# GpSimd without arithmetic in the expert blocks of a two-block transformer

## Chip, core and metric

The kernel runs on one core of one Trainium2 chip. The metric is the device time of one execution in microseconds (us). Engines are named as in the profile: PE (TensorE, matrix products), DVE (VectorE), ACT (ScalarE), POOL (GpSimd) and SP (SyncE, which only issues transfers). PEclk is the granted clock of PE as a share of full speed.

## What is computed

A first block (two layers of three token mixers and a feed-forward of width 2816, on 256 tokens of width 1024) is followed by a second block of two layers. Each of these holds an attention of the 256 latent tokens, together with 256 context tokens, and an expert layer with 16384 experts. Everything is in float32.

```
first_block, per layer:  x += concat(rwkv7(h), dilated(h), mla(h)) @ w_out
                         x += (silu(h @ w_gate) * (h @ w_up)) @ w_down        # h = rms_norm(x)
second_block, per layer: x += g1 * attention(...) @ w_o
                         x += g2 * peer_ffn(h2)                               # latents
  layer 0 only:          xc += cg2 * peer_ffn(h2c)                            # context

def peer_block(hb, w_q, sub_keys, u_tab, v_tab):
    q1, q2 = halves of (hb @ w_q) per head                    # 8 heads
    v1, i1 = top_k(q1 @ sub_keys[0].T, 16); v2, i2 = top_k(q2 @ sub_keys[1].T, 16)
    top_s, pos = top_k(v1[:, None] + v2[None, :], 16)         # 16 of 256 pairs
    expert = (i1 * 128 + i2)[pos];  g = softmax(top_s)
    u = u_tab[expert]                                         # 128 rows per token
    w = g * gelu(einsum('nhkd,nd->nhk', u, hb))
    return einsum('nhk,nhkd->nd', w, v_tab[expert])
```

## The kernel before

**Products.** A float32 product is made of three PE products of parts: a tensor is split into `hi` (ACT, L177) and `lo = src - hi` (L181), and `mm3` (L184 to L191) adds hi*hi, hi*lo and lo*hi. `split` puts the subtraction on VectorE or, with `eng2="g"`, on GpSimd.

**Feed-forward (`ffn`, L509).** For each of 22 tiles of the width, gate and up products, then the activation (`ffact`, L526). A second loop over the 22 tiles splits the activation (`ffak`, hi on ACT and lo on GpSimd, L540) and half of the tiles of `w_down` on VectorE and GpSimd in turn (L538), and accumulates into four banks of PSUM.

**Experts of the context tokens (`peer_gather`, L1394), layer 0.** For each of two blocks of 128 tokens there are 128 gathers of u rows (`ug`, L1425; each brings 128 rows of 4 KB), each followed by a dot product with `hm`: on GpSimd and ACT (L1415 and L1416) or as one operation on VectorE (L1418). `dot` chooses: in block 0 the first 60 and every third after the 118th go to GpSimd, in block 1 every third. Then 128 gathers of v rows (`vg`, L1449) feed small products `pv` (L1454). This work runs beside the second feed-forward, attention 0 and the layer 0 experts of the latents. The u rows pass through four buffers, from the 174th on through two.

**Experts of the latents (`Dense`, L1500).** All 16384 experts are computed for all 256 tokens, in parts (four of 32 tiles in layer 0, two of 64 in layer 1), and weighted by a mostly empty matrix. `u_part`: a tile `u_raw` is loaded, split (hi on ACT L1564, lo by columns on GpSimd and VectorE L1567: 256 of 1024 columns on GpSimd in the first two parts of layer 0, 512 in the others), multiplied (`aT`, L1580 to L1582), and passed through gelu to `d_A`. `w_part`: one-hot matrices `o` (L1621, L1623) and `og` (L1626) on VectorE, a product `gps` on PE (L1630), and the result multiplied into `d_A` (L1632). `v_part`: a tile `v_raw` is loaded and split (hi on ACT L1649, lo half on GpSimd L1650 and half on VectorE L1651), a row of `d_A` is split (`w_hi`, `w_lo`, L177 and L181), and PE accumulates `acc` (L1664). `mesh` interleaves the loops. In layer 0 the order is u0 with the routing, u1 beside w0, v0 beside w1, u2, v1 beside w2, u3, v2 beside w3, v3. In layer 1 it is u0 with the routing, u1 beside w0, v0 beside w1, v1.

**Order.** A scheduler places the instructions of each engine by priorities (`n.rank`, `issue_after`) and its own model of time. Every engine runs its list in order: an instruction that waits holds all behind it on its engine. Gathers stand in POOL's list, loads of tiles in SP's.

Names that the prediction uses: `qn` (L1171) is a normalised query of attention 0, `h2xv` (L1097) belongs to the norm that ends attention 0, `d_gT` (L1603) is the end of the routing.

Of the kernel before, what the change touches and what calls it, by code (L numbers as in the profile page):

```python
# [10 lines left out]
F32 = mybir.dt.float32  # L11
F32R = mybir.dt.float32r
# [4 lines left out]
AF = mybir.ActivationFunctionType  # L17
ALU = mybir.AluOpType
# [3 lines left out]
P = 128  # L22
D = 1024
S = 256
KD = D // P
L = 2
DFF = 2816
KF = DFF // P
# [216 lines left out]
def part(pair, *idx):  # L245
    return tuple(t[(slice(None),) + idx] for t in pair)
# [51 lines left out]
class First:  # L298
# [207 lines left out]
                xs = x[:, b, hf * 512 : (hf + 1) * 512]  # L506
                nc.vector.tensor_tensor(xs, pss[hf][b], xs, op=ALU.add)

    def ffn(self, l, x, after=None, more=None):  # L509

        nc, n, a = self.nc, self.n, self.a
        hT, _ = self.norm_T(x, self.vcol("ffn_norm_g", l, 8), "hT2")
        if after:
            after()
        act = self.zones["x"].tile([P, KF, S], F32, name="ffact")
        for c in range(KF):
            ps = self.psum("pgu")
            for i, name in enumerate(("ffn_w_gate", "ffn_w_up")):
                w = self.w.load(a[name][l, c], KD, P, "wgu")
                for k in range(KD):  # L520
                    n.mm3(ps[:, i * S : (i + 1) * S], part(w, k), part(hT, k), k == 0, k == KD - 1)
            th = self.t([P, S], "ffth")
            nc.scalar.activation(th, ps[:, :S], AF.Tanh, scale=0.5)
            nc.vector.tensor_scalar(th, th, 0.5, 0.5, op0=ALU.mult, op1=ALU.add)
            nc.vector.tensor_tensor(th, ps[:, :S], th, op=ALU.mult)
            nc.vector.tensor_tensor(act[:, c], ps[:, S:], th, op=ALU.mult)  # L526
        wd = a["ffn_w_down"][l].rearrange("(k p) c -> p k c", p=P)
        pss = [self.psum(f"pd{i}") for i in range(4)]
        for k in range(KF):
            ws = self.w if more is None or k % 2 else more  # L530
            if k % 4 < 2:
                w = part(ws.load(wd[:, k : k + 1], 1, D, "wd"), 0)
            else:
                if k % 2 == 0:
                    two = self.zones["x"].pair([P, 2, D], "wd2")
                w = part(two, k % 2)
                raw = ws.plain(wd[:, k : k + 1], 1, D, "wd")
                n.split(raw[:, 0], *w, eng2="gv"[k % 2])  # L538
            ak = self.z.pair([P, S], "ffak")
            n.split(act[:, k], *ak, eng2="g")  # L540
            for b in range(2):
                for hf in range(2):
                    n.mm3(pss[2 * b + hf], part(ak, slice(b * P, (b + 1) * P)), part(w, slice(hf * 512, (hf + 1) * 512)), k == 0, k == KF - 1)
        for b in range(2):
            for hf in range(2):
                xs = x[:, b, hf * 512 : (hf + 1) * 512]
                nc.vector.tensor_tensor(xs, pss[2 * b + hf], xs, op=ALU.add)
# [438 lines left out]
class Second:  # L986
# [408 lines left out]
    def peer_gather(self, slots, rows, out, gp, vp, act0, hm0):  # L1395
# [3 lines left out]
        n, nc = self.n, self.nc  # L1399
# [7 lines left out]
        def u_rows(b):  # L1407
            hm = self.t([P, D], "hm") if b else hm0
            nc.gpsimd.dma_start(hm, rows[b])
            act = self.t([P, P], "act") if b else act0  # L1410

            def dot(j, u):
                o = act[:, j : j + 1]
                if j < EARLY if b == 0 and j < EARLY + GATHERS else j % POOL_DOTS == 0:
                    nc.gpsimd.tensor_tensor(u, u, hm, op=ALU.mult)  # L1415
                    nc.scalar.activation(u, u, AF.Copy, accum_out=o)  # L1416
                else:
                    nc.vector.tensor_tensor_reduce(out=u, in0=u, in1=hm, scale=1.0, scalar=0.0, op0=ALU.mult, op1=ALU.add, accum_out=o)  # L1418

            for j in range(P):  # L1420
                if b == 0 and j == SOON:
                    hm = self.t([P, D], "hm")
                    nc.gpsimd.dma_start(hm, rows[b])
                u = row(j, "ug")
                nc.gpsimd.indirect_dma_start(out=u, out_offset=None, in_=ut, in_offset=bass.IndirectOffsetOnAxis(ap=slots[b][0][:, j : j + 1], axis=0))  # L1425
                dot(j, u)
                yield
            gl = self.gelu(act, [P, P], "ga")
            w = self.t([P, P], "gw_")
            nc.vector.scalar_tensor_tensor(w, gl, 0.5, slots[b][2][:, b], op0=ALU.mult, op1=ALU.mult)  # L1430
            ps = self.psumt()
            nc.tensor.transpose(ps[:, 0:P], w, n.ident)
            wTs[b] = self.t([P, P], "wT")
            nc.scalar.activation(wTs[b], ps[:, 0:P], AF.Copy)
# [68 lines left out]
class Dense:  # L1503
# [9 lines left out]
    def __init__(self, net, ctx, x, h, l, col, parts, banks, raw):  # L1513
        tc = net.tc
        self.n, self.nc, self.a = net, net.nc, net.a
        self.x, self.l, self.col = x, l, col
        self.hh, self.hl = h
        self.pw, self.pr = None, raw
        self.parts = parts
        self.low = ((2, 2, 4, 4), (4, 4))[l]  # L1520
        self.first = [sum(parts[:i]) for i in range(len(parts))]
        self.pa = ctx.enter_context(tc.tile_pool(name=f"d_a{l}", bufs=1, reuse_waits="tile"))
        self.i = 0
        self.pr2 = None if l else ctx.enter_context(tc.tile_pool(name=f"d_s{l}", bufs=RAWS, reuse_waits="tile"))
        self.pu = ctx.enter_context(tc.tile_pool(name=f"d_u{l}", bufs=2 if l else SPLITS, reuse_waits="tile"))
        self.po = ctx.enter_context(tc.tile_pool(name=f"d_o{l}", bufs=2, reuse_waits="tile"))
        self.pp = ctx.enter_context(tc.tile_pool(name=f"d_p{l}", bufs=banks, space=PSUM, reuse_waits="tile"))
# [26 lines left out]
    def u_part(self, f, A):  # L1554
        nc, n, H = self.nc, self.n, self.parts[f]
        cols = self.a["u_columns"][self.l]

        def split(i):
            u = self.raw([P, KD, P], "u_raw")
            nc.sync.dma_start(u, cols[self.first[f] + i])  # L1560
            uh = self.pu.tile([P, KD, P], F32R, tag="hi", name="u_hi")
            ul = self.pu.tile([P, KD, P], F32R, tag="lo", name="u_lo")
            q = self.low[f]
            nc.scalar.activation(uh, u, AF.Copy)  # L1564
            for e, o, m in ((nc.gpsimd, 0, q), (nc.vector, q, KD)):
                if o < m:
                    e.tensor_tensor(ul[:, o:m], u[:, o:m], uh[:, o:m].bitcast(F32), op=ALU.subtract)  # L1567
            return uh, ul

        ahead = [split(0)]  # L1570
        pa = None
        for i in range(H):
            if i + 1 < H:
                ahead.append(split(i + 1))
            uh, ul = ahead.pop(0)
            if i % 2 == 0:
                pa = self.psum("aT")
            o = pa[:, (i % 2) * S : (i % 2 + 1) * S]
            for k in range(KD):
                nc.tensor.matmul(o, uh[:, k], self.hh[:, k], start=k == 0, stop=False)  # L1580
                nc.tensor.matmul(o, uh[:, k], self.hl[:, k], start=False, stop=False)  # L1581
                nc.tensor.matmul(o, ul[:, k], self.hh[:, k], start=False, stop=k == KD - 1)  # L1582
            if i % 2 or i == H - 1:
                i0 = i - i % 2
                nc.scalar.activation(A[:, i0 : i + 1].rearrange("p i n -> p (i n)"), pa[:, : (i + 1 - i0) * S], AF.Gelu_apprx_tanh)
            yield
# [51 lines left out]
    def v_part(self, f, W, starts, stops):  # L1638

        nc, n, H = self.nc, self.n, self.parts[f]  # L1640
        vv = self.a["peer_v_2"][self.l].rearrange("(p j) d -> p j d", j=P)
        ready = []
        for i in range(H):
            i2 = self.first[f] + i
            v = self.raw([P, D], "v_raw")
            nc.sync.dma_start(v, vv[:, i2])
            vh = self.pu.tile([P, D], F32R, tag="hi", name="v_hi")
            vl = self.pu.tile([P, D], F32R, tag="lo", name="v_lo")
            nc.scalar.activation(vh, v, AF.Copy)  # L1649
            nc.gpsimd.tensor_tensor(vl[:, 0:512], v[:, 0:512], vh[:, 0:512].bitcast(F32), op=ALU.subtract)  # L1650
            nc.vector.tensor_tensor(vl[:, 512:], v[:, 512:], vh[:, 512:].bitcast(F32), op=ALU.subtract)  # L1651
            wh = self.po.tile([P, S], F32R, tag="wh", name="w_hi")
            wl = self.po.tile([P, S], F32R, tag="wl", name="w_lo")
            self.split(W[:, i], wh, wl)
# [49 lines left out]
EARLY = 60  # L1704
# [1 line left out]
MORE = 56  # L1706
UFIRST = EARLY + GATHERS + MORE - P
LOW = "gv"
POOL_DOTS = 3
GATHER_CLASSES = ((32, 8), (512, 5), (1024, 2), (4096, 1))  # L1710
ATTN_CLASSES = (
    ((32, 24), (256, 8), (1024, 8), (2048, 4), (4096, 3), (8192, 4)),
# [5 lines left out]
def build(tc, aps, out):  # L1718
    with ExitStack() as ctx:
# [93 lines left out]
        def gather_on(count):  # L1813

            with n.rank(at[0]), tc.issue_after(n.last.ins):
                for _ in itertools.islice(gather, count):
                    pass
                at[0] = tc.cur_priority

        with f.scope("f1", FFN_ZONES, 6, {"w": 6}, "v", 4):  # L1820
            f.ffn(1, x, lambda: gather_on(GATHERS))
        fx.close()
        for l in range(L):
            last = l == L - 1
# [128 lines left out]
```

## Time and profile before

| | |
|---|---|
| median of 3 runs | 3541.01 us (3537.23 to 3547.21) |
| profiled execution | 3555.65 us, span 3553.9 us, mean granted clock 0.935 |
| busy share of the span | PE 88%, DVE 74%, POOL 54%, ACT 40% |
| data moved | 761.46 MB, mean 214 GB/s |
| second feed-forward | 887 to 1125 us |
| attention 0 (layer 0) | 1125 to 1395 us |
| layer 0 experts | 1395 to 2525 us |
| attention 1 | 2525 to 2705 us |
| layer 1 experts | 2705 to 3553 us |

The stages are read from the timeline, where the names of a stage begin and end. A row of the windows view has the window and its length, then for each of PE, PEld, DVE, ACT and POOL the busy time (and the number of instructions), then PEclk, the share of time that the DMA engines were busy, and the rate in GB/s. Busy shares over the whole span hide that the stages have different limits, so the stages are read one by one.

### The profile page before, as it was taken

The page shows a single profiled execution, that of the slowest core. Times are in us where ns is not written, and L with a number is a line of the kernel's source. Part 1 is how long each engine was busy: PE and PEld are TensorE (multiplying, and loading weights), DVE is VectorE, ACT ScalarE, POOL GpSimd, SP SyncE. Part 2 cuts the span into 40 slices and gives each one's busy share as a digit, 9 for nine tenths or more (in the row PEclk, how much of TensorE's full clock was granted, in tenths as well). Part 3 has the DMA queues.
Part 4 walks back from the last instruction along what each step waited for, and adds up shares of the span by engine and source line. Part 5 has one row for each costly group of instructions (what it writes and reads, how often), then busy time and mean ns, then how long its engine had stood idle before and what let it go on. Part 6 is the DMA issues. An engine that isn't in the chain of part 4 may idle for free. (4 is left out here: it accounts for less than half of the span.)

```text
span 3553.9 us, 58408 instructions
## 1 busy us (share of the span) xinstructions
PE 3114.9 (88%) x22044; PEld 2575.2 (72%) x22044; DVE 2635.4 (74%) x5055; ACT 1426.0 (40%) x2195; POOL 1920.3 (54%) x1368
## 2 busy tenths in 40 slices
PE   8979997688896768879878899999888899999999
PEld 6758895566795558867557658756668899986887
DVE  5647789774897789999875784675677826789777
ACT  4234543443543454433323333323454343443454
POOL 2113228656667576667557657666211465544665
PEclk9999999899898879989989999999899999999999
DMA  6555554667897567778768779878423454544555
GB/s 205 174 165 162 161 161 155 205 218 238 301 331 248 174 224 243 240 276 312 247 232 306 274 265 322 306 280 322 143 68 118 154 178 155 167 155 137 183 191 172
DMA packets 260970, 761.46 MB, mean 214 GB/s; under 512 B 26064, under 2 KB 81424, under 8 KB 260688
## 3 DMA queue, kind: packets, MB, share of 16 engines
q1 hardware_dynamic: 127856, 410.50, 34.5%
q0 software_dynamic: 79456, 289.18, 23.7%
q10 hardware_dynamic: 53376, 58.05, 5.0%
q8 instruction: 173, 2.83, 0.3%
q14 instruction: 109, 0.89, 0.1%
HBM read 753.44 MB, written 4.19 MB: 213 GB/s over the span
## 5 line engine op out<-in xcount | busy, mean ns | idle before, releaser
L1582 PE MATMUL aT<-h_hi,u_lo 128*128 128x256 f32 x2048 | 595.6, 292 | 53.6 <-POOL u_lo L1567 26.7
L1580 PE MATMUL aT<-h_hi,u_hi 128*128 128x256 f32 x2048 | 595.0, 291 | 7.5 <-ACT u_hi L1564 6.8
L1581 PE MATMUL aT<-h_lo,u_hi 128*128 128x256 f32 x2048 | 588.4, 288 | 0.0
L1650 POOL TENSOR_TENSOR v_lo<-v_raw,v_hi 128x512 fp32r<-128x512 f32 x256 | 398.7, 1564 | 247.3 <-ACT v_hi L1649 223.4
L1567 POOL TENSOR_TENSOR u_lo<-u_raw,u_hi 128x512 fp32r<-128x512 f32 (+1 forms) x256 | 362.7, 1425 | 293.0 <-ACT u_hi L1564 284.8
L1425 POOL DMA_INDIRECT ug<-in_peer_u,slot_e x256 | 311.8, 1218 | 285.5 <-DVE act L1418 122.2
L1649 ACT ACTIVATE v_hi<-v_raw 128x1024 fp32r<-128x1024 f32 x256 | 270.8, 1059 | 477.6 <-issue 222.0
L1564 ACT ACTIVATE u_hi<-u_raw 128x1024 fp32r<-128x1024 f32 x256 | 269.5, 1058 | 477.4 <-PE aT L1581 216.2
L1582 PEld LDWEIGHTS aT<-h_hi,u_lo 128*128 128x128 f32 x2048 | 400.8, 196 | 68.3 <-DVE u_lo L1567 30.5
L1580 PEld LDWEIGHTS aT<-h_hi,u_hi 128*128 128x128 f32 x2048 | 402.6, 197 | 14.7 <-ACT u_hi L1564 9.0
L1581 PEld LDWEIGHTS aT<-h_lo,u_hi 128*128 128x128 f32 x2048 | 402.4, 196 | 4.2 <-issue 4.2
L1664 PE MATMUL acc<-v_hi,w_lo 128*128 128x512 f32 x1024 | 339.2, 413 | 60.2 <-DVE w_lo L181 59.5
L1567 DVE TENSOR_TENSOR u_lo<-u_raw,u_hi 128x512 fp32r<-128x512 f32 (+1 forms) x256 | 262.5, 1027 | 163.1 <-ACT u_hi L1564 138.7
L1449 POOL DMA_INDIRECT vg<-in_peer_v,slot_eT x256 | 262.6, 1026 | 142.1 <-PE pv L1454 59.7
L1664 PE MATMUL acc<-v_lo,w_hi 128*128 128x512 f32 x1024 | 331.4, 405 | 0.1
L1664 PE MATMUL acc<-v_hi,w_hi 128*128 128x512 f32 x1024 | 308.6, 411 | 5.2 <-ACT w_hi L177 5.2
L1415 POOL TENSOR_TENSOR ug<-ug,hm 128x1024 f32<-128x1024 f32 x106 | 263.4, 2489 | 65.9 <-DMA ug<-in_peer_u,slot_e 62.3
L1651 DVE TENSOR_TENSOR v_lo<-v_raw,v_hi 128x512 fp32r<-128x512 f32 x256 | 203.5, 795 | 116.0 <-ACT v_hi L1649 102.9
L1664 PEld LDWEIGHTS acc<-v_hi,w_lo 128*128 128x128 f32 x1024 | 192.4, 195 | 119.6 <-DVE w_lo L181 74.7
L181 DVE TENSOR_TENSOR w_lo<-d_A,w_hi 128x256 fp32r<-128x256 f32 x256 | 264.0, 1033 | 3.7 <-ACT w_hi L177 3.5
L1418 DVE CUSTOM_DVE_ANT_0 ug<-ug,hm 128x1024 f32<-128x1024 f32 x150 | 212.3, 1423 | 37.9 <-DMA ug<-in_peer_u,slot_e 35.4
L1664 PEld LDWEIGHTS acc<-v_lo,w_hi 128*128 128x128 f32 x1024 | 199.2, 196 | 45.9 <-issue 2.0
(659 smaller groups left out, 7539.3 us busy)
## 6 DMA issues: line engine op xcount, KB each, us to landing
u_raw<-in_u_columns SPq DMA_DIRECT2D x256, 512.0 KB
v_raw<-in_peer_v SPq DMA_DIRECT2D x256, 512.0 KB
adaw<-in_ada_w ACTq DMA_DIRECT2D x96, 512.0 KB
wgu<-in_ffn_w_gate SPq DMA_DIRECT2D x44, 512.0 KB
wgu<-in_ffn_w_up SPq DMA_DIRECT2D x44, 512.0 KB
wd<-in_ffn_w_down SPq DMA_DIRECT2D x44, 512.0 KB
wpq<-in_peer_w_q SPq DMA_DIRECT2D x32, 512.0 KB
wqkv<-in_w_qkv SPq DMA_DIRECT2D x24, 512.0 KB
```

Source lines behind the costliest of these rows:

```text
L181: e.tensor_tensor(lo, src, hi.bitcast(F32), op=ALU.subtract)
L1415: nc.gpsimd.tensor_tensor(u, u, hm, op=ALU.mult)
L1425: nc.gpsimd.indirect_dma_start(out=u, out_offset=None, in_=ut, in_offset=bass.IndirectOffsetOnAxis(ap=slots[b][0][:, j : j + 1], axis=0))
L1449: loads.append(nc.gpsimd.indirect_dma_start(out=four[q], out_offset=None, in_=vt, in_offset=bass.IndirectOffsetOnAxis(ap=slots[b][1][:, to ...
L1564: nc.scalar.activation(uh, u, AF.Copy)
L1567: e.tensor_tensor(ul[:, o:m], u[:, o:m], uh[:, o:m].bitcast(F32), op=ALU.subtract)
L1580: nc.tensor.matmul(o, uh[:, k], self.hh[:, k], start=k == 0, stop=False)
L1581: nc.tensor.matmul(o, uh[:, k], self.hl[:, k], start=False, stop=False)
L1582: nc.tensor.matmul(o, ul[:, k], self.hh[:, k], start=False, stop=k == KD - 1)
L1649: nc.scalar.activation(vh, v, AF.Copy)
L1650: nc.gpsimd.tensor_tensor(vl[:, 0:512], v[:, 0:512], vh[:, 0:512].bitcast(F32), op=ALU.subtract)
L1664: nc.tensor.matmul(self.acc[2 * b + hf], x[:, bs], y[:, hf * 512 : (hf + 1) * 512], start=s0, stop=s1)
```

## The change

Three things are changed. The second feed-forward (`early=True`) splits its activations as they are made, into two tiles that stay (a new zone "y" of 22528 bytes per partition holds the lo part), and all its `w_down` splits are VectorE's. In `peer_gather` only the first 60 dots of block 0 stay on GpSimd; the 46 later ones that were GpSimd's and ACT's become VectorE's. In `Dense` each u and v tile has its lo part made by one VectorE operation on 128x1024 through `split` (L181) in place of a VectorE and a GpSimd share: 256 u and 256 v operations of GpSimd vanish. `self.low` and `POOL_DOTS` go.

```diff
-    def ffn(self, l, x, after=None, more=None):
+    def ffn(self, l, x, after=None, more=None, early=False):
...
-        act = self.zones["x"].tile([P, KF, S], F32, name="ffact")
+        if early:
+            act = self.zones["x"].tile([P, KF, S], F32R, name="ffact_hi"), self.zones["y"].tile([P, KF, S], F32R, name="ffact_lo")
+        else:
+            act = self.zones["x"].tile([P, KF, S], F32, name="ffact")
...
-            nc.vector.tensor_tensor(act[:, c], ps[:, S:], th, op=ALU.mult)
+            if early:
+                nc.vector.tensor_tensor(th, ps[:, S:], th, op=ALU.mult)
+                n.split(th, *part(act, c))
+            else:
+                nc.vector.tensor_tensor(act[:, c], ps[:, S:], th, op=ALU.mult)
...
-                n.split(raw[:, 0], *w, eng2="gv"[k % 2])
-            ak = self.z.pair([P, S], "ffak")
-            n.split(act[:, k], *ak, eng2="g")
+                n.split(raw[:, 0], *w, eng2="v" if early else "gv"[k % 2])
+            if early:
+                ak = part(act, k)
+            else:
+                ak = self.z.pair([P, S], "ffak")
+                n.split(act[:, k], *ak, eng2="g")
...
-                if j < EARLY if b == 0 and j < EARLY + GATHERS else j % POOL_DOTS == 0:
+                if b == 0 and j < EARLY:
                     nc.gpsimd.tensor_tensor(u, u, hm, op=ALU.mult)
                     nc.scalar.activation(u, u, AF.Copy, accum_out=o)
                 else:
...
-            q = self.low[f]
-            nc.scalar.activation(uh, u, AF.Copy)
-            for e, o, m in ((nc.gpsimd, 0, q), (nc.vector, q, KD)):
-                if o < m:
-                    e.tensor_tensor(ul[:, o:m], u[:, o:m], uh[:, o:m].bitcast(F32), op=ALU.subtract)
+            self.split(u, uh, ul)
...
-            nc.scalar.activation(vh, v, AF.Copy)
-            nc.gpsimd.tensor_tensor(vl[:, 0:512], v[:, 0:512], vh[:, 0:512].bitcast(F32), op=ALU.subtract)
-            nc.vector.tensor_tensor(vl[:, 512:], v[:, 512:], vh[:, 512:].bitcast(F32), op=ALU.subtract)
+            self.split(v, vh, vl)
...
-        with f.scope("f1", FFN_ZONES, 6, {"w": 6}, "v", 4):
-            f.ffn(1, x, lambda: gather_on(GATHERS))
+        with f.scope("f1", dict(FFN_ZONES, y=((22528, 1),)), 6, {"w": 6}, "v", 4):
+            f.ffn(1, x, lambda: gather_on(GATHERS), early=True)
```

The scheduler then orders the lists anew from the second feed-forward on. POOL has 325 rows fewer. On SP, ACT and POOL the first loads and copies of attention 0 (`qkg`, `sink`, `c_attn`, `kT`, `vt`) now stand behind the second feed-forward, whose extra zone takes their place in SBUF. VectorE's dots stand further ahead: the number of them in its list ahead of the last `qn` of attention 0 is 58 before and 58 after, ahead of `h2xv` 79 and 109, ahead of `d_gT` 113 and 171, ahead of the 64th u tile's split 124 and 190; in all there are 150 and 196.

The end of POOL's list, from attention 1 on (`qo` and `nr_y` are attention 1's last operations there). Before:

```order
L1181 TENSOR_TENSOR rm_25364<-qn,c_attn 128x256
L1182 TENSOR_TENSOR qo<-rm_25363,rm_25364 128x8x32
L212 TENSOR_TENSOR nr_y<-h2xv,mhalf 128x2
L1567 TENSOR_TENSOR u_lo<-u_raw,u_hi 128x512 x128
L1650 TENSOR_TENSOR v_lo<-v_raw,v_hi 128x512 x128
L1949 UNCONDITIONAL_BRANCH
L1949 ISA
```

After:

```order
L1191 TENSOR_TENSOR rm_25022<-qn,c_attn 128x256
L1192 TENSOR_TENSOR rm_25023<-qn,c_attn 128x256
L1193 TENSOR_TENSOR qo<-rm_25022,rm_25023 128x8x32
L212 TENSOR_TENSOR nr_y<-h2xv,mhalf 128x2
L1952 UNCONDITIONAL_BRANCH
L1952 ISA
```

POOL has nothing to do in the whole of layer 1's experts.

VectorE in layer 0 beside v0 and w1, where `v_lo` and `w_lo` are what `acc` needs, and `o`, `og` and `d_A` are w1's. Before:

```order
L1621 TENSOR_TENSOR o_17701<-iota_64,d_iT 128x1024
L1626 TENSOR_TENSOR og<-o_17703,d_gT 128x256 x2
L1651 TENSOR_TENSOR v_lo<-v_raw,v_hi 128x512
L1418 ISA ug,act<-ug,hm 128x1024
L1418 ISA act 128x1
L181 TENSOR_TENSOR w_lo<-d_A,w_hi 128x256
L1623 TENSOR_TENSOR o_17799<-iota_64,d_iT 128x256
L1632 SCALAR_TENSOR_TENSOR d_A<-gps,d_A 128x32x8
```

After:

```order
L1627 TENSOR_TENSOR o_17543<-iota_64,d_iT 128x1024
L1632 TENSOR_TENSOR og<-o_17545,d_gT 128x256 x2
L181 TENSOR_TENSOR v_lo<-v_raw,v_hi 128x1024
L181 TENSOR_TENSOR w_lo<-d_A,w_hi 128x256
L1429 ISA ug,act<-ug,hm 128x1024
L1429 ISA act 128x1
L1629 TENSOR_TENSOR o_17639<-iota_64,d_iT 128x256
L1638 SCALAR_TENSOR_TENSOR d_A<-gps,d_A 128x32x8
```

One operation of twice the width stands in the place of VectorE's half; the order is otherwise alike, with the dot behind `w_lo`.

VectorE in the core of attention 0 (`am` and `az` are maxima and sums of the softmax, `pTh` its transposed weights, `zw` a copy for the v rows). Before:

```order
L1418 ISA ug,act_3944<-ug,hm 128x1024
L1418 ISA act_3944 128x1
L1216 TENSOR_REDUCE am<-as 128x1
L1227 RECIPROCAL az<-az 128x1
L1418 ISA ug,act_3944<-ug,hm 128x1024
L1418 ISA act_3944 128x1
L1221 TENSOR_SCALAR am<-am 128x1
L198 COPY pTh<-stp 128x4x128
L1216 TENSOR_REDUCE am<-as 128x1
```

After:

```order
L1429 ISA ug,act<-ug,hm 128x1024
L1429 ISA act 128x1
L1429 ISA ug,act<-ug,hm 128x1024
L1429 ISA act 128x1
L1429 ISA ug,act<-ug,hm 128x1024
L1429 ISA act 128x1
L1429 ISA ug,act<-ug,hm 128x1024
L1429 ISA act 128x1
L1456 COPY zw_11289<-wT 128x4
L1456 COPY zw_11290<-wT 128x4
L1227 TENSOR_REDUCE am<-as 128x1
L198 COPY pTh<-stp 128x4x128
```

Each dot is two rows. Where before single dots stood between the steps of the softmax, now there are up to four in a row.

## Rows read from the trace of the kernel before

**Rows 1.** Windows of the span: us, busy us (xinstructions), PEclk, DMA share, GB/s
```profile
925.00:1060.00 135.00, 131.05 (x1067) 129.49 (x1066) 129.99 (x167) 68.86 (x101) 84.23 (x52) 0.98 0.91 324
1225.00:1320.00 95.00, 64.62 (x265) 47.36 (x266) 76.02 (x130) 51.85 (x100) 70.01 (x47) 0.83 0.67 226
1395.00:1550.00 155.00, 112.84 (x844) 107.63 (x845) 150.96 (x442) 63.87 (x81) 98.42 (x79) 0.89 0.69 230
1680.00:1860.00 180.00, 143.67 (x1059) 98.17 (x1061) 146.27 (x265) 49.99 (x76) 104.68 (x87) 0.89 0.72 241
1860.00:2000.00 140.00, 123.26 (x945) 106.58 (x938) 81.61 (x75) 49.02 (x62) 104.08 (x87) 0.94 0.86 304
2000.00:2140.00 140.00, 119.88 (x928) 78.47 (x924) 116.00 (x228) 44.22 (x68) 86.28 (x72) 0.94 0.76 265
2850.00:3153.00 303.00, 300.23 (x2820) 296.48 (x2820) 176.61 (x269) 125.35 (x147) 163.16 (x96) 0.99 0.52 167
3153.00:3310.00 157.00, 145.43 (x1015) 109.12 (x1014) 149.74 (x239) 57.60 (x84) 65.15 (x43) 0.96 0.42 139
```

**Rows 2.** Timeline of one tile, last part of layer 1
```profile
3380.11 0.69 DVE L1651 TENSOR_TENSOR v_lo<-v_raw,v_hi 128x512 fp32r<-128x512 f32 x1 [0.60 <-ACT v_hi L1649]
...
3380.15 1.79 POOL L1650 TENSOR_TENSOR v_lo<-v_raw,v_hi 128x512 fp32r<-128x512 f32 x1 [0.93 <-ACT v_hi L1649]
...
3380.72 1.51 DVE L181 TENSOR_TENSOR w_lo<-d_A,w_hi 128x256 fp32r<-128x256 f32 x1
```

**Rows 3.** Single operations on VectorE, whole span: ns min/median/max
```profile
L181 DVE TENSOR_TENSOR w_lo<-d_A,w_hi x256: 404/668/6835, 1684.4 to 3541.2; 128x256 fp32r<-128x256 f32 x128
...
L1651 DVE TENSOR_TENSOR v_lo<-v_raw,v_hi x256: 676/692/3481, 1676.2 to 3540.6; 128x512 fp32r<-128x512 f32 x128
...
L1621 DVE TENSOR_TENSOR o<-iota,d_iT x192: 673/681/5575, 1547.6 to 3290.6; 128x1024 f16<-128x1024 bf16 x192
...
L181 DVE TENSOR_TENSOR wgu_lo<-wgu,wgu_hi x66: 1205/1222/4092, 256.0 to 1045.2; 128x1024 fp32r<-128x1024 f32 x66
...
L1418 DVE CUSTOM_DVE_ANT_0 ug<-ug,hm x150: 1196/1215/5139, 927.6 to 2054.5; 128x1024 f32<-128x1024 f32 x150
```

**Rows 4.** Groups by line, VectorE, 1680 to 1860 us
```profile
L1621 DVE TENSOR_TENSOR o<-iota,d_iT 128x1024 f16<-128x1024 bf16 x33 | 35.0, 1061 | 0.0
...
L181 DVE TENSOR_TENSOR w_lo<-d_A,w_hi 128x256 fp32r<-128x256 f32 x34 | 34.0, 1004 | 1.9 <-ACT w_hi L177 1.7
...
L1651 DVE TENSOR_TENSOR v_lo<-v_raw,v_hi 128x512 fp32r<-128x512 f32 x31 | 25.6, 827 | 1.2 <-ACT v_hi L1649 1.2
```

**Rows 5.** Waits of PE, 1680 to 2525 us: us, times, longest
```profile
PE acc L1664 <- DVE w_lo L181: 52.1, 27, 5.6
PE gps L1630 <- DVE og L1626: 16.9, 6, 5.9
PE aT L1582 <- POOL u_lo L1567: 16.7, 7, 3.4
```

**Rows 6.** Waits of PE, 3153 to 3310 us
```profile
PE acc L1664 <- DVE w_lo L181: 7.4, 8, 1.4
```

**Rows 7.** Waits of PE, 887 to 1125 us (second feed-forward)
```profile
PE pd L190 <- POOL wd_lo L181: 4.5, 2, 3.1
```

**Rows 8.** Timeline of VectorE, three places that mark stages
```profile
1217.58 1.13 DVE L1171 SCALAR_TENSOR_TENSOR qn<-sps,qr_y,qkg 128x128 f32<-128x128 f32 x4
...
1314.28 0.17 DVE L1097 TENSOR_SCALAR h2xv<-h2xv 128x2 f32<-128x2 f32 x1
...
1541.34 0.28 DVE L1603 CAST d_gT<-d_gf 128x256 f16<-128x256 f32 x1
```

**Rows 9.** Waits of VectorE, 1125 to 1550 us
```profile
DVE ug L1418 <- DMA ug<-in_peer_u,slot_e: 35.4, 20, 5.8
```

**Rows 10.** Gathers of u rows in two windows: ns min/median/max, first and last start
```profile
L1425 POOL DMA_INDIRECT ug<-in_peer_u,slot_e x71: 935/1010/1978, 1125.7 to 1391.4; - x71
...
L1425 POOL DMA_INDIRECT ug<-in_peer_u,slot_e x28: 935/1076/2857, 1395.8 to 1548.9; - x28
```

More of the change, by code (lines that the diff above doesn't have):

```diff
@@ L1519, in __init__ @@
         self.parts = parts
-        self.low = ((2, 2, 4, 4), (4, 4))[l]
         self.first = [sum(parts[:i]) for i in range(len(parts))]
@@ L1708 @@
 LOW = "gv"
-POOL_DOTS = 3
 GATHER_CLASSES = ((32, 8), (512, 5), (1024, 2), (4096, 1))
```

## The prediction

> **What bounds the kernel now.** I read the windows by stage first [rows 1], because PE's 88% of the span is a mean over stages that differ. In layer 1's u part (2850 to 3153 us) PE works 300.2 of 303 us at a clock of 0.99: nothing that VectorE or GpSimd does can shorten it. In layer 0's experts it is otherwise. From 1680 to 1860 us PE works 143.7 of 180 us at a clock of 0.89, while VectorE works 146.3; from 1395 to 1550 us VectorE works 151.0 of 155 and PE only 112.8. Then I read what PE waits for there [rows 5]: from 1680 to 2525 us it waits 52.1 us for VectorE's `w_lo`, 16.9 for `og` and 16.7 for GpSimd's `u_lo`, 85.7 us together.
>
> Why is VectorE late? The single operations [rows 3] and the means of a stage [rows 4] answer: `w_lo` takes 0.404 us at best and 1.004 in the mean of 1680 to 1860, `o` 0.681 in the median and 1.061 there. The timeline of one tile shows what stretches them [rows 2]. GpSimd's `v_lo` runs from 3380.15 to 3381.94; the `w_lo` of VectorE that starts inside it lasts 1.51 us and ends 0.29 us after it. So VectorE is stretched while a GpSimd subtraction runs, and GpSimd needs 1.79 us for the half tile that VectorE does in 0.69.
>
> Last I read the gathers: between 1125 and 1550 us VectorE waits 35.4 us, in 20 places, for a u row that has not landed [rows 9]. The changed order puts more dots just there.
>
> **The change part by part.** The sum is made against the profiled execution (3555.65 us), which lies 14.6 us above the median of the runs; the result is carried to the median.
>
> *Splits, layer 0, 1680 to 1860.* What goes is the stretch: `o` 33 x (1.061 - 0.681) = 12.5, `w_lo` 34 x (1.004 - 0.404) = 20.4, `v_lo` 31 x (0.827 - 0.692) = 4.2, 37 us together [rows 3, 4]. What comes is the other half of each tile: a whole 128x1024 subtraction takes 1.22 us on VectorE (the row of `wgu_lo`), the half 0.69, so 31 x 0.53 = 16.4 us. VectorE gets 21 us lighter, and as dots have moved ahead some more: from 146 to about 120 of 180 us. PE idles 36 us here. I take 30 of them back, and 5 more because a PE that does not pause holds a higher clock: 0.89 in this row against 0.94 at 123 of 140 us and 0.98 at 131 of 135 [rows 1]. Term: -35.
>
> *The rest of 1680 to 2525.* Of the 85.7 us of waits [rows 5], 36 lie in the stage above (its idle time), 16.7 are GpSimd's `u_lo` in the u parts, and the remaining 33 lie in v1, v2 and v3 beside their w parts. For `u_lo` VectorE has room: 81.6 of 140 us between 1860 and 2000, and 29 tiles x 0.53 = 15 us more; its waits go nearly all: -15. For the others the same exchange of stretch against width holds: -30 of 33. Together -45.
>
> *Splits, layer 1.* v0 beside w1 waits 7.4 us for `w_lo` [rows 6] and idles 11.6 [rows 1]; 43 x 0.53 = 23 us come onto a VectorE with 149.7 of 157 us, and about as much stretch goes. Bounds +15 and -11, taken: -10, because here too GpSimd's overlap goes wholly. The u part and v1 are PE's: 0; what hides the 0.53 us per tile is a VectorE busy 176.6 of 303 us. Without that cover it would be 64 x 0.53 = 34 us.
>
> *Second feed-forward.* In its first loop (925 to 1060 us) PE works 131.1 and VectorE 130.0 of 135 us [rows 1]. 22 lo splits of 128x256 come to VectorE, at the 0.40 of `w_lo` [rows 3] 9 us, a few of which PE will feel. In its second loop 11 `w_down` splits x 1.22 = 13 us come to VectorE, and the 4.5 us that PE waits for GpSimd's `wd_lo` go [rows 7]. The first loads of attention 0 now come behind this stage; they are small beside 232 to 324 GB/s of tiles. Bounds -5 and +10, taken: 0.
>
> *Dots, attention 0.* The three marks [rows 8] make two stretches of the list: `qn` at 1217.6, `h2xv` at 1314.3, `d_gT` at 1541.3 us. In the first, 96.7 us, stand 21 VectorE dots before and 51 after: 30 x 1.29 (1.215 and 0.077 for its second row) = 39 us more on a VectorE that works 76.0 of 95 us between 1225 and 1320. It has 19 us free, and loses some stretch with the GpSimd dots. A dot also waits for its gather, and holds the softmax behind it. Bounds 0 and +39, taken +15.
>
> *Dots, u0 and routing.* In the second stretch, 227 us, stand 34 before and 62 after: 28 x 1.29 = 36 us more, and 32 u splits that are wider by a quarter of a tile, some 10 us, on a VectorE with 4 us free [rows 1]. Against it stand the stretch that goes and PE's 42 idle us here, which are not all on the path. Bounds 0 and +46, taken +20. Later VectorE has fewer dots: that is in the -35.
>
> Sum: -35 - 45 - 10 + 0 + 15 + 20 = -55. 3555.65 - 55 = 3500.7 in the profiled execution, 3486 at the median. With the terms at their bounds, from -91 + 0 - 11 - 5 = -107 to +70 (-40, half of the layer 0 splits, + 15 + 10 + 39 + 46); all ends at once are unlikely, and I give this case 3440 to 3525.
>
> **Rivals.**
>
> *A. PE reaches its floor.* If the stretch was all that held layer 0's experts, PE's idle time from 1395 to 2525 returns nearly whole (42 + 86 us) and its clock with it (143.7 us at 0.89 would be some 131 at 0.98, so about 15 over the stages), while dots fit the freed time: -140 + 10 = -130, thus 3411. For it: VectorE, not PE, is the fuller engine in both waiting stages. Against it: DMA. 1680 to 2000 moved 241 x 180 + 304 x 140 = 86 MB in 320 us, 269 GB/s; the best window shows 324 [rows 1], which allows 265 us there, but only just so when gathers lie in the way.
>
> *B. The dots hold VectorE (slower).* VectorE's list is in order, so a dot whose row has not landed stops the softmax, the routing and the u splits behind it. Place: from `h2xv` to `d_gT`, where the rows pass through two buffers from the 174th on, so a gather starts only when the dot two before it is done. Before, gathers came at (1548.9 - 1395.8) / 27 = 5.7 us each there, and at 3.8 in 1125 to 1395 [rows 10]. 62 dots at 5.7 us need 353 us and not 227: +126; with +15 before and -90 behind it +51, thus 3592. It decides from about (227 + 90 - 15) / 62 = 4.9 us per row. Against it: those gathers waited for VectorE rather than for memory (the gather itself is 1.08 us of GpSimd, and DMA is busy 0.69 of the time at 230 GB/s; 28 rows more of 0.52 MB are 15 MB, 65 GB/s over 227 us). For it: the 35.4 us of waiting in 20 places [rows 9] came with a third of these dots.
>
> *C. VectorE gets the work and no relief (slower).* If the stretch were VectorE's own or came from the gathers, the three v parts beside w parts would pay 96 x 0.53 = 51 us, the dots +35, and only the 16.7 us of `u_lo` waits would go: +69, thus 3610. Rows 2 speak against it: the 1.51 us `w_lo` lies inside a GpSimd operation and ends with it. The Trainium skill ("Perfetto Trace Analysis", section "Optimizing Scalar/DVE Operations") says that where VectorE is saturated, giving work to ScalarE or even GpSimd may make sense, which speaks against this change, since it gives work to a VectorE at 146 of 180 us. The same paragraph adds that GpSimd and VectorE share an SBUF read port, so that moving work between those two might not help; by that half the time is the forecast's, by the first half it is C's. The trace agrees with the second.
>
> **How the numbers follow.** The forecast's case 0.66, A 0.12, B 0.16, C 0.06. About 0.3% (11 us) is what a measurement of this kernel can tell from no change. Of the forecast's case 0.61 is faster by more, 0.04 the same, 0.01 slower; A is faster; B, whose price slides with the pace of the gathers, gives 0.03 faster, 0.03 same, 0.10 slower; C 0.06 slower. Faster 0.76, same 0.07, slower 0.17. The range leaves out the low half of A and the upper part of B and C: 3410 to 3565.
>
> **What would show it.** In the profile after, GpSimd has no `u_lo` or `v_lo`, and its busy share falls to about a fifth to a third. `w_lo` on VectorE should have a mean near its best, 0.40 to 0.45 us, and `o` 0.68; if they stay near 1.0, C holds. PE's idle time in v0 beside w1 should fall from 36 to under 8 us and its clock there rise over 0.93. The waits of VectorE for `ug` from DMA should grow from 35 to 60 or 90 us; over 150 is B. The time from `qn` to `h2xv` should be about 112 us, from `h2xv` to `d_gT` about 247. The forecast fails if the stages from 1680 to 2525, 845 us now, take over 800, or if attention 0 and the routing grow by more than 80.

## The result and the profile after

The changed kernel takes 3417.9 us in the median (3416.0 to 3429.5), the kernel before 3541.2: ratio 0.966 (0.963 to 0.968), 123 us faster. The sign was forecast, the size was not: the forecast was 55 us, with a range down to 3410, and the time came out near that of rival A (3411), which had 12 in 100.

Stages in us, each from mark to mark in the timelines (feed-forward: between the two residual sums; attention 0: last `qn` to `h2xv`; routing: to `d_gT`; u1: to the end of the 64th `u_lo`; then to the end of each 32nd `v_lo` or `u_lo`). "Before" is the profile of the rows above, "again" a second profile of the same kernel. The last four columns are runs told below: the splits alone, the dots alone, and two runs with arithmetic on GpSimd whose results nothing reads.

| stage | before | again | after | splits | dots | dots+idle | idle 512 |
|---|---|---|---|---|---|---|---|
| second feed-forward | 225.9 | 228.1 | 209.0 | 229.1 | 228.3 | 212.1 | 212.4 |
| attention 0 | 95.7 | 96.5 | 115.5 | 97.3 | 115.8 | 95.6 | 116.4 |
| routing | 227.3 | 229.8 | 245.5 | 239.3 | 239.9 | 236.6 | 242.0 |
| u1 | 132.3 | 130.7 | 125.6 | 124.2 | 126.1 | 131.1 | 130.2 |
| v0 and w1 | 174.7 | 175.5 | 128.4 | 130.0 | 151.9 | 158.1 | 141.1 |
| u2 | 133.4 | 136.1 | 115.7 | 118.7 | 115.4 | 127.3 | 112.1 |
| v1 and w2 | 152.7 | 149.7 | 128.5 | 120.9 | 138.4 | 145.0 | 134.8 |
| u3 | 113.8 | 112.3 | 115.0 | 113.7 | 115.6 | 111.9 | 111.7 |
| v2 and w3 | 155.4 | 137.9 | 129.4 | 131.9 | 134.1 | 136.5 | 135.9 |
| v3 | 111.7 | 110.5 | 88.2 | 101.4 | 93.7 | 108.2 | 91.3 |
| v0 to v3 together | 841.6 | 822.0 | 705.2 | 716.5 | 749.2 | 787.0 | 726.9 |
| layer 1, u0 and u1 | 476.5 | 471.9 | 477.4 | 477.2 | 477.0 | 501.1 | 501.3 |
| layer 1, v0 and w1 | 218.4 | 214.5 | 201.0 | 201.0 | 213.8 | 225.3 | 225.3 |

The windows of the changed kernel (columns as in [rows 1]): the second loop of the second feed-forward, attention 0, the routing, `d_gT` to the end of v3, v0 beside w1, and u2.

```profile
1060.00:1124.00 64.00, 60.45 (x269) 49.81 (x268) 53.94 (x78) 22.68 (x30) 26.32 (x22) 1.00 0.80 288
1208.00:1323.00 115.00, 72.75 (x265) 49.29 (x265) 96.54 (x188) 41.19 (x78) 67.70 (x56) 0.83 0.81 278
1323.00:1568.00 245.00, 172.06 (x1300) 165.17 (x1300) 216.22 (x642) 78.20 (x98) 81.61 (x64) 0.86 0.72 238
1568.00:2399.00 831.00, 820.66 (x6839) 624.25 (x6840) 554.38 (x1132) 301.27 (x408) 305.22 (x280) 0.99 0.88 315
1694.00:1822.00 128.00, 127.03 (x1091) 85.62 (x1093) 106.59 (x251) 44.25 (x65) 56.30 (x48) 1.00 0.90 326
1822.00:1938.00 116.00, 116.00 (x954) 96.62 (x947) 47.46 (x64) 41.70 (x49) 44.30 (x43) 1.00 0.93 337
```

And of the kernel before, the second loop of the feed-forward, the routing, and `d_gT` to the end of v3, which answer to the first, third and fourth row:

```profile
1052.00:1138.00 86.00, 67.35 (x270) 53.05 (x268) 68.02 (x75) 29.84 (x50) 71.32 (x49) 0.88 0.76 262
1314.00:1541.00 227.00, 173.38 (x1300) 166.00 (x1300) 217.37 (x586) 96.11 (x133) 149.08 (x108) 0.89 0.68 229
1541.00:2515.00 974.00, 869.41 (x6837) 653.68 (x6838) 698.54 (x1155) 320.05 (x444) 651.29 (x547) 0.94 0.81 286
```

The same 6840 matmuls stand in both long windows. PE was idle 105 us of 974 and is idle 10 of 831; and the matmuls themselves took 869 us at a clock of 0.94 and take 821 at 0.99. So 94 us came from idle time and 49 from PE's busy time, at the higher clock. Against the second profile of the kernel before (953 us, of which PE works 855) it is 87 and 35. From v0 on PE hardly pauses: it works 127.03 of 128 us in v0 beside w1 and 116.00 of 116 in u2.

One tile of layer 1's v1 [rows 2], then `w_lo` over the span [rows 3], and PE's waits from 1694 to 2399 us [rows 5], after:

```profile
3247.83 1.23 DVE L181 TENSOR_TENSOR v_lo<-v_raw,v_hi 128x1024 fp32r<-128x1024 f32 x1 [1.16 <-ACT v_hi L177]
3248.97 0.42 DVE L181 TENSOR_TENSOR w_lo<-d_A,w_hi 128x256 fp32r<-128x256 f32 x1
```

```profile
L181 DVE TENSOR_TENSOR w_lo<-d_A,w_hi x256: 404/417/426, 1705.0 to 3406.7; 128x256 fp32r<-128x256 f32 x128
```

```profile
PE acc L1668 <- ACT w_hi L177: 1.0, 1, 1.0
```

The longest `w_lo` fell from 6.8 us to 0.43, and 52.1 us of PE's waits for it are gone. The waits of VectorE for gathers from 1119 to 1568 us [rows 9], and the gathers of the routing, after and (from 1314 to 1541 us) before [rows 10]:

```profile
DVE ug L1429 <- DMA ug<-in_peer_u,slot_e: 50.4, 41, 4.0
```

```profile
L1436 POOL DMA_INDIRECT ug<-in_peer_u,slot_e x61: 936/939/2938, 1322.0 to 1564.2; - x61
```

```profile
L1425 POOL DMA_INDIRECT ug<-in_peer_u,slot_e x51: 935/1112/2857, 1314.0 to 1540.2; - x51
```

Twice as many waits, but 15 us more in all; from `h2xv` to `d_gT` a gather comes every 4.0 us, where the kernel before had one every 4.5.

### The profile page after: what moved, and what is told of

Same layout as the page of the kernel before. It is cut to its first block, busy times and chain, and to the rows that moved or that the text cites. A ratio compares the mean times of both kernels' runs of the same rounds, so it can differ in the third digit from the quotient of the medians.

```text
span 3417.6 us, 56879 instructions
## 1 busy us (share of the span) xinstructions
PE 3054.9 (89%) x22044; PEld 2537.6 (74%) x22044; DVE 2453.8 (72%) x5174; ACT 1376.3 (40%) x2103; POOL 1016.5 (30%) x783
## 4 chain that ended last, share of the span: by engine, by line
PE 61%; DVE 18%; issue 8%; DMA 7%; POOL 3%; ACT 2%; SPq 0%; POOLq 0%; DVEq 0%; ACTq 0%
PE acc L1668 19%; PE aT L1588 5%; PE aT L1586 5%; PE aT L1587 5%; DMA ug<-in_peer_u,slot_e 4%; PE pv L1465 3%; PE gps L1636 2%; DMA adaw<-in_ada_w 2%; POOL ug L1436 2%; DVE u_lo L181 2%; PE sps L189 2%; PE sps L190 2%; PE sps L191 2%; DVE ug L1429 1%; PE pgu L191 1%
## 5 line engine op out<-in xcount | busy, mean ns | idle before, releaser
L181 DVE TENSOR_TENSOR u_lo<-u_raw,u_hi 128x1024 fp32r<-128x1024 f32 x256 | 312.2, 1220 | 206.2 <-ACT u_hi L177 206.0
L181 DVE TENSOR_TENSOR v_lo<-v_raw,v_hi 128x1024 fp32r<-128x1024 f32 x256 | 312.8, 1222 | 162.8 <-ACT v_hi L177 160.7
L1460 POOL DMA_INDIRECT vg<-in_peer_v,slot_eT x256 | 280.2, 1095 | 379.0 <-PE pv L1465 278.0
L1668 PE MATMUL acc<-v_lo,w_hi 128*128 128x512 f32 x1024 | 318.1, 391 | 0.0
L1668 PE MATMUL acc<-v_hi,w_hi 128*128 128x512 f32 x1024 | 286.1, 398 | 1.0 <-ACT w_hi L177 1.0
L1429 DVE CUSTOM_DVE_ANT_0 ug<-ug,hm 128x1024 f32<-128x1024 f32 x196 | 239.9, 1229 | 64.4 <-DMA ug<-in_peer_u,slot_e 63.9
L1668 PEld LDWEIGHTS acc<-v_hi,w_hi 128*128 128x128 f32 x1024 | 185.1, 188 | 34.5 <-ACT w_hi L177 1.1
L191 PE MATMUL pgu<-hT_hi,wgu_lo 128*128 128x256 f32 x704 | 201.7, 287 | 7.3 <-DVE wgu_lo L181 5.7
L189 PE MATMUL pgu<-hT_hi,wgu_hi 128*128 128x256 f32 x704 | 200.2, 285 | 0.7 <-ACT wgu_hi L177 0.7
L190 PE MATMUL pgu<-hT_lo,wgu_hi 128*128 128x256 f32 x704 | 199.6, 284 | 0.0
```

Source lines behind the costliest of these rows:

```text
L181: e.tensor_tensor(lo, src, hi.bitcast(F32), op=ALU.subtract)
L189: mm(out, a[0], b[0], start=start, stop=False)
L190: mm(out, a[0], b[1], start=False, stop=False)
L191: mm(out, a[1], b[0], start=False, stop=stop)
L1460: loads.append(nc.gpsimd.indirect_dma_start(out=four[q], out_offset=None, in_=vt, in_offset=bass.IndirectOffsetOnAxis(ap=slots[b][1][:, to ...
L1668: nc.tensor.matmul(self.acc[2 * b + hf], x[:, bs], y[:, hf * 512 : (hf + 1) * 512], start=s0, stop=s1)
```

## Experiments

Each kernel is timed beside the kernel before on its own chip, so ratios are compared. Theory 1: GpSimd's arithmetic stretched VectorE, and without it PE is at its floor (the time that its own products take when it does not wait). Theory 2: the context's work, moved ahead, freed the late stages.

**Splits alone**: the `u_part` and `v_part` hunks of the diff.

> The u and v splits whole on VectorE alone; dots and second feed-forward as before. Theory 1 (the GpSimd subtractions stretched VectorE; without them PE reaches its floor at full clock in layer 0's experts): the stages from the end of u1 to the end of v3, 841 us before and 705 after, come to 705 to 740, layer 1 gains 17, attention 0 and the second feed-forward stay: 3405 to 3440. Theory 2 (the context's dots and v rows moved ahead freed the late stages, v3 above all): u1 to v3 comes to about 770 (the forecast's sizes for the splits), v3 stays near 110, total 3450 to 3480.

Ratio 0.965 (0.963 to 0.968), v0 to v3 716.5 us. Theory 1's size, and as much as the whole change gained.

**Dots alone**: the `dot` line.

> The late dots on VectorE alone; splits and second feed-forward as before. Theory 1: attention 0 and the routing grow by some 38 us as in the changed kernel, and 110 us of GpSimd multiplications fewer in the rest give back 20 to 45: 3530 to 3560, v1 and v2 parts beside w stay over 140 us. Theory 2: u1 to v3 falls by 60 to 90 us, v3 comes to 88: 3480 to 3520.

Ratio 0.984 (0.980 to 0.987), v0 to v3 749.2 us: theory 2's size. PE still waits 30.1 us for `w_lo` there. The gains of splits and dots in v0 to v3 (125 and 92 us against the first profile of the kernel before, 106 and 73 against the second) do not add: the whole change gained 136 and 117.

**Feed-forward alone**: `early=True`.

> The second feed-forward's early split alone. Both theories: the stage (end of the second mixers' residual to the end of the feed-forward's, 226 us before, 209 after) falls by 12 to 17 us, nothing else moves: 3524 to 3530. If its gain in the changed kernel came from the changed order of attention 0's loads or of the gathers rather than from the early split, under 5 us: 3536 to 3541.

Ratio 0.991 (0.989 to 0.993); the stage takes 213.1 us, 13 less as expected, but the total fell by 32 us, more than either theory had. The rest lies in v0 to v3 (804 us), where this kernel has the same operations as the kernel before; that kernel's own two profiles differ there by 20 us, so what the early split did to this stretch stays open.

**Splits and feed-forward, dots on GpSimd as before**:

```diff
-                if b == 0 and j < EARLY:
+                if j < EARLY if b == 0 and j < EARLY + GATHERS else j % POOL_DOTS == 0:
```

> The changed kernel with the late dots on GpSimd and ACT again. Theory 1: attention 0 and the routing take 20 to 38 us less than in the changed kernel, the remaining GpSimd multiplications cost 0 to 30 in u1 to v3: 3390 to 3420, as fast as the changed kernel or faster. Theory 2: 3435 to 3470, slower than the changed kernel.

Ratio 0.959 (0.958 to 0.961), better than the changed kernel, as theory 1 had it: attention 0 takes 95.2 us, v0 to v3 714.9. So in the changed kernel, whose splits are gone from GpSimd, moving the dots costs 20 us in attention 0 and 15 in the routing and brings 10 in v0 to v3.

**Dots divided**: GpSimd's third only in block 0 and up to the 76th of block 1.

```diff
+                if j < EARLY if b == 0 and j < EARLY + GATHERS else j % POOL_DOTS == 0 and (b == 0 or j < 76):
```

> The changed kernel, with every third of the late dots on GpSimd and ACT again as long as they stand in attention 0 and the routing (block 0, and block 1 up to the 76th), and VectorE's after that. Theory 1 (GpSimd's arithmetic costs only where VectorE's stretch makes PE wait; late in layer 0 PE is at its floor): attention 0 96 us and the routing 230 as in the run with splits and feed-forward, u1 to v3 705 to 712 as in the changed kernel: 3385 to 3398. If the dots cost by their number wherever GpSimd does them: 3400 to 3410, between the two.

Ratio 0.956 (0.954 to 0.958), the lowest, but its interval meets that of the run before it, and the two medians (3398.3 and 3399.2 us) differ by 1 us. Its stages are those of the run before it within 4 us except u2 (118.8 for 109.0), and v0 to v3 takes 716.1, not 705 to 712: taking these last dots off GpSimd did not help.

**Late dots alone**: the kernel before with the same `dot` line.

> The kernel before, with only the late dots behind the 76th of block 1 (17 GpSimd multiplications) moved to VectorE; splits and feed-forward as before. If the gain of the run with the dots alone (u1 to v3 749 us) came from GpSimd's multiplications beside the expert parts: u1 to v3 760 to 800, total 3490 to 3515. If it came from the context's work being moved ahead, out of the late parts: u1 to v3 800 to 840, v3 near 110 us, total 3520 to 3545.

Ratio 0.991 (0.989 to 0.993), v0 to v3 807.7, v3 115.6 us. Against the second profile's 822.0 this is little, so these 17 multiplications are the smaller part of what the dots alone gained. In v3 one reason for the rest can be seen: with all late dots moved 48 of the context's 144 `pv` products are left there (5.8 us), here all 144 (17.3 us). For the other stages no reason was shown.

**Idle subtractions**: the changed kernel, GpSimd subtracting beside each split into a tile that nothing reads.

```diff
+        for i in range(q):
+            h = hi[:, i * S : (i + 1) * S].bitcast(F32)
+            self.nc.gpsimd.tensor_tensor(self.scr, h, h, op=ALU.subtract)
```

> The changed kernel, and beside each u and v split GpSimd subtracts a piece of the tile's hi part from itself into a scratch tile that nothing reads (as many columns as its share was before, in pieces of 128x256): its arithmetic without anyone waiting for its result. Theory 1 (the arithmetic itself stretches VectorE): w_lo's mean goes from about 0.43 back to 0.7 to 1.5 us, PE waits again, u1 to v3 from 705 to 760 to 850 us, total 3480 to 3570. Rival (PE waited for GpSimd's late halves and for lists in order, not for a stretched VectorE): w_lo stays under 0.5, total 3415 to 3430.

Ratio 0.981 (0.979 to 0.984): some 55 us of the gain are gone though nothing reads what GpSimd makes. `w_lo`'s mean is 0.708 us, as theory 1 said; but v0 to v3 takes 725.7 us, below its numbers, and 38 us of the loss lie in layer 1 (501.4 us in the u parts, 215.2 in v0 beside w1). The work is not wholly idle: it reads the hi part, and a later hi part goes into the same buffer, so ScalarE waits 181.7 us in 79 places for these subtractions.

**Idle zeros**: the same with `memset(self.scr, 0.0)` behind each hi part.

> The same as the run with idle subtractions, but GpSimd only fills the scratch tile with zeros (128x256, behind each split's hi part): it writes and reads nothing. If what stretches VectorE is GpSimd reading SBUF: w_lo under 0.5 us, total 3412 to 3425 as the changed kernel. If any instruction of GpSimd that touches SBUF does it: w_lo 0.6 to 1.2, total 3450 to 3540.

Ratio 0.964 (0.962 to 0.966), that of the changed kernel. `w_lo` in this run, over the span:

```profile
L181 DVE TENSOR_TENSOR w_lo<-d_A,w_hi x256: 407/417/425, 1700.9 to 3403.3; 128x256 fp32r<-128x256 f32 x128
```

960 fills stretch nothing, and ScalarE never waits for them; subtractions do stretch. The Trainium skill ("SBUF — State Buffer", section "Who interferes with whom") says that a VectorE instruction with two SBUF inputs contends with a GpSimd instruction that reads SBUF, not with one that only writes it; the two runs agree.

**Idle subtractions in one piece** of GpSimd's former size (128x512):

```diff
+        h = hi[:, : q * S].bitcast(F32)
+        self.nc.gpsimd.tensor_tensor(self.scr[:, : q * S], h, h, op=ALU.subtract)
```

The scratch tile `scr` is bfloat16 here. In the first two u parts of layer 0 the piece is 128x256, as GpSimd's share was.

> As the run with idle subtractions, but in one piece as large as GpSimd's share was before (128x512, 128x256 in the first two u parts of layer 0), written as bfloat16 to the scratch tile. Theory 1 (a VectorE operation is held for as long as the GpSimd operation that it meets, so the size of the piece sets the price): w_lo's mean 0.9 to 1.3 us where it was 0.71 with small pieces, u1 to v3 765 to 840 us where it was 726, total 3530 to 3590. Rival (PE waited for GpSimd's results and for lists in order; the stretch alone is a small part): u1 to v3 715 to 740, total 3480 to 3500.

Ratio 0.990 (0.987 to 0.992). `w_lo` is back at 0.985 us in the mean, 1.03 before, and yet v0 to v3 takes only 726.9 us: the rival's numbers. Theory 1 was right on how long VectorE is held and wrong on what it costs. One pair of this run:

```profile
3403.30 2.01 POOL L1556 TENSOR_TENSOR scr<-v_hi 128x512 bf16<-128x512 f32 x1 [0.42 <-ACT v_hi L177]
3404.34 1.26 DVE L181 TENSOR_TENSOR w_lo<-d_A,w_hi 128x256 fp32r<-128x256 f32 x1
```

The subtraction ends at 3405.31 us and `w_lo` 0.29 us later, the same distance as in [rows 2]. It is so for all 172 `w_lo` of this run that take over 0.6 us, for all 180 of the run with small pieces, and for all 128 of the kernel before: each ends 0.28 or 0.29 us after a GpSimd subtraction.

These idle subtractions cost 22 us in v0 to v3, and 24 each in layer 1's u parts and v0. In the u parts (2583 to 3084 us) VectorE's load does not explain it: VectorE works 361 of 501 us, and `u_lo` takes 1.240 us in the mean where the changed kernel has 1.220. ScalarE waits there for the reading of its hi part:

```profile
ACT u_hi L177 <- POOL scr L1556: 31.9, 19, 3.2
```

What this wait and the stretch each cost was not separated.

**v alone, u alone**: one hunk of the splits each.

> The kernel before with the v splits alone whole on VectorE. Theory 1: the v parts beside w parts lose w_lo's waits and come to 125 to 132 us each, u2 keeps the 17 us of waits for GpSimd's u_lo, layer 1 gains 17: u1 to v3 735 to 765, total 3440 to 3475. If the gain is one of GpSimd's list as a whole, half of it: 3475 to 3490.

> The kernel before with the u splits alone whole on VectorE. Theory 1: u2 comes to 116 us, the v parts beside w parts keep w_lo's waits and stay at 140 to 170: u1 to v3 780 to 815, layer 1 as before, total 3500 to 3530. If the gain is one of GpSimd's list as a whole, half of it: 3475 to 3490.

Ratios 0.976 (0.974 to 0.978) and 0.985 (0.983 to 0.987); v0 to v3 743 and 770 us. Beside 822 to 842 before that is some 80 to 100 and 50 to 70: more together than the 105 to 125 of both. The first is theory 1's size; the second misses it (780 to 815, and 3480 us where 3500 to 3530 was expected). With v alone, u2 keeps its waits for GpSimd's `u_lo` (15.0 us) and takes 140; with u alone it takes 110 and PE still waits 28.6 us for `w_lo`.

**The kernel before again.**

> The kernel before once more, for a second profile of it: how far its stages differ from one execution to the next. The run with the early feed-forward alone had u1 to v3 at 804 us and the first profile 841; if this stretch varies by execution, it lies here between 800 and 845 while layer 1 stays within 2 us; if 841 is what the kernel always needs, within 5 us of it. Total 3530 to 3560.

3524.8 us, v0 to v3 822.0: 20 us less than in the first profile, and the total lies 5 us under the 3530 to 3560 expected. So v0 to v3 varies by execution. Layer 1 moved by more than the 2 us named, 4 to 5 us in each of two stages.

**Dots and idle subtractions.** Theory 3: PE waited for lo halves that stood in GpSimd's list behind dots. Theory 4: dots and subtractions together hold VectorE.

```diff
+                if j < EARLY if b == 0 and j < EARLY + GATHERS else j % POOL_DOTS == 0:
...
+        self.nc.gpsimd.tensor_tensor(self.scr[:, : q * S], h, h, op=ALU.subtract)
```

> The run with splits and feed-forward (late dots on GpSimd as before, u1 to v3 715 us), with the idle subtractions of the size of GpSimd's share before (which alone took the changed kernel's u1 to v3 from 705 to 727). GpSimd then does all the arithmetic that it did before, in the same list with the gathers and dots, but neither PE nor VectorE waits for its subtractions. Theory 3 (in the kernel before PE waited for lo halves that stood in GpSimd's list behind dots and gathers): the two costs add, 715 + 22: u1 to v3 730 to 750, w_lo's longest about 4 us, total 3445 to 3475. Theory 4 (dots and subtractions back to back on GpSimd hold VectorE for several of them at a time): u1 to v3 780 to 830 as in the kernel before, w_lo up to 5 to 7 us, total 3500 to 3540.

Ratio 0.994 (0.993 to 0.996): of the 0.041 gained by splits and feed-forward 0.035 are lost, to results that nothing reads. Some 46 us of it lie in layer 1, whose u parts take 501 us where the kernel before takes 476. v0 to v3 takes 787.0 us, 72 more than without the idle work, where the changed kernel lost 22 to it. Theory 3's sum (730 to 750) fails and theory 4's size holds, but not what was to show it: `w_lo`'s longest is 1.7 us, not 5 to 7. What the runs show in place of it is VectorE's load beside v0 and w1, in the run without idle work, with it, and in the changed kernel with idle work in one piece:

```profile
1657.00:1784.00 127.00, 123.05 (x1042) 86.37 (x1041) 123.49 (x254) 49.84 (x76) 67.81 (x54) 1.00 0.93 337
```

```profile
1673.00:1831.00 158.00, 135.74 (x1039) 92.89 (x1032) 152.09 (x255) 49.63 (x75) 111.60 (x88) 0.90 0.79 270
```

```profile
1702.00:1843.00 141.00, 131.40 (x1083) 88.56 (x1085) 137.72 (x252) 44.64 (x66) 105.84 (x82) 0.96 0.85 300
```

VectorE works 123.5 us where the stage's floor on PE is 127: nothing is lost. At 137.7 and 152.1 it is the bound (98% and 96% of the stage), and the stage takes what VectorE takes. In this stage the stretch costs only what it lifts VectorE above PE's floor. The stage has 31 of the 72 us. v1 beside w2 has 18, with VectorE again busy 136.3 of 145 us. u2 has 18 too, but there VectorE works 73 of 127 us and ScalarE waits for the idle reading:

```profile
ACT u_hi L177 <- POOL scr L1556: 32.6, 10, 5.7
```

The last 35 to 55 us to the kernel before were not taken apart; 17 to 21 of them are PE's waits for GpSimd's `u_lo` there [rows 5].

## Why the prediction was wrong

**What bounds it: right.** VectorE, stretched by GpSimd's subtractions, held PE in layer 0's experts where v and w parts run side by side: there VectorE is the bound again when the subtractions are put back without a reader, and with fills it is not. Of the 107 to 127 us that splits and early feed-forward gain in v0 to v3, 72 are lost this way, some of them to ScalarE's waits; the rest was not reproduced.

**Splits beside v0 and w1, -35: measured -46.** VectorE fell to 106.6 us (about 120 was forecast).

**The rest of 1680 to 2525, -45: measured -90.** This is the step that failed. u2 gave 17.7 (15 forecast), v1 beside w2 24.2, v2 beside w3 26.0 and v3 23.5, together 74 where 30 of 33 us of waits were priced. Against the second profile the stretch gave 70, the difference lying mostly in v2 beside w3 (8.5 us there). Two things were missed. First, "5 more because a PE that does not pause holds a higher clock" was allowed to one stage, while 49 us (35 against the second profile) between `d_gT` and the end of v3 came from PE's busy time. In v0 beside w1 one `acc` product, here of before and after, fell from 0.449 to 0.409 us:

```profile
L1664 PE MATMUL acc<-v_hi,w_lo 128*128 128x512 f32 x124 | 45.3, 449 | 23.0 <-DVE w_lo L181 23.0
```

```profile
L1668 PE MATMUL acc<-v_hi,w_lo 128*128 128x512 f32 x118 | 38.9, 409 | 0.0
```

Second, v3 was already PE's (108 of 111 us), but 144 `pv` products of the context stood in it, 17.3 us, which now run before it. About 20 of the 136 us of v0 to v3 are only the spread between two profiles of the kernel before; against the second, the gain is 117 where 80 were forecast.

**Second feed-forward, 0: measured -17.** Its first loop (912 to 1052 us before, 915 to 1060 after) grew by 5 us, as its working had it, but the second fell from 86 to 64: the row of waits named 4.5 us, while PE's idle time was 19 us and its clock 0.88. Again the floor counted, not the named wait.

**Layer 1, -10: measured -17** (-13 against the second profile), all in v0 beside w1; the u parts took 477 us for 476 and 472, and v1 stayed.

**Dots, +15 and +20: measured +20 and +18.** The marks are 115.5 and 245.5 us apart (112 and 247 forecast). The waits for gathers rose to 50.4 us (60 to 90 forecast). u1, which had no term, gave 7.

**Rivals.** A named the right end, PE at its floor, and its time is right in part by luck. Its 140 us stand against 143 measured from `d_gT` to the end of v3 (122 against the second profile), but 42 of them were idle time of the routing that did not come back: PE idles 73 us in the routing after, 54 before. Its 10 us of cost were 38 in attention 0 and the routing, set off by 34 gained in the feed-forward and layer 1, which it did not have. It was put at 12 in 100 because of DMA; the windows after move 326 and 337 GB/s where 324 was the best seen, so what had been read as a limit was only the rate asked for. B failed: gathers came every 4.0 us, under the 4.9 from which it decides. Its 5.7 us per gather, said of the whole way from `h2xv` to `d_gT`, was read from the last 155 us alone; over the whole it was 4.5 before the change, so B could have been put lower from the start. C failed: `w_lo`'s median is 0.417 us.

## What to carry to other kernels

Price a stage by each engine's floor, its count of instructions times their best durations, and take the longest: here, once the bound was lifted, the time fell to the next floor, with the clock, and not by the sum of the waits that a view names. A floor does not see everything: layer 1's u parts lost 24 us to the idle subtractions with VectorE working 361 of 501 us and PE only 4 us longer than without them. Two edits that each lift the same bound do not add, so try each alone: here one of the three parts, the dots, cost more than it gave once the splits were moved. Arithmetic on GpSimd is not free on VectorE even when nothing reads its result, and work that only reads a buffer still keeps that buffer from its next writer.

## What had not been expected

GpSimd's fills (960 of 128x256, 302 us) left VectorE's 0.417 us untouched, while subtractions of the same tiles raised it to 0.708, and twice as large ones to 0.985: the price on VectorE goes with the size of the GpSimd operation, not with GpSimd being busy (the small subtractions keep it busy 957 us, the large ones 801). The cost in time is not linear: the same idle subtractions took 22 us of v0 to v3 where VectorE had room, and 72 where dots were on GpSimd too.
